# A decoder layer on one core: the second SwiGLU's first two weights split into the places of later sums, the post-norm's load moved behind the weights', two loads moved to the other ring

## The chip, the cores and the metric

The kernel runs on one core of one Trainium2 chip. A core has a matrix engine (PE), three engines for elementwise work (DVE, ACT and POOL), an engine that only issues transfers here (SP) and 16 DMA engines. Each engine works through its own list of instructions in the order of the program and waits where it needs another's result. The metric is the device time of one execution in microseconds, the median of several runs.

## The reference

One decoder layer on x of 512 tokens by 1024, float32: a SwiGLU feed-forward, a mixer of two kinds of recurrent heads, and a second SwiGLU, each between a norm before it and a norm behind it.

```python
x = x + 0.5 * rms_norm(swiglu_ffn(rms_norm(x, norm_pre[l, 0]), ffn1_w_in[l], ffn1_w_out[l]), norm_post[l, 0])
mixed = token_mixer(rms_norm(x, norm_pre[l, 1]), w_mix_in[l], ...)
x = x + rms_norm(mixed, norm_post[l, 1])
x = x + 0.5 * rms_norm(swiglu_ffn(rms_norm(x, norm_pre[l, 2]), ffn2_w_in[l], ffn2_w_out[l]), norm_post[l, 2])

def swiglu_ffn(x, w_in, w_out):
    gate, up = jnp.split(x @ w_in, 2, axis=-1)
    return (jax.nn.silu(gate) * up) @ w_out
```

`w_in` is 1024 by 5632 (gate and up, 2816 columns each), `w_out` 2816 by 1024. The token mixer ends with a product `mix @ w_out` of 1024 by 1024. The result is compared in float32.

## The kernel before

**Precision.** PE multiplies float32 operands in a rounded form (fp32r). Each operand is therefore split into a high part, which is its rounded copy, and a low part, which is the rest. ACT makes the high part (`L273`, 128 x 1024), DVE the low part (`L275`, a subtraction); three matmuls, high by high, high by low and low by high, stand for one. The mixer's output weights are scaled at the same time (`L278` on ACT, `L281` on DVE, two halves of 128 x 512 for each weight).

**Products.** The input product of a SwiGLU is done by a scheme of seven products (p1 to p7) in place of eight for each pair t of column tiles (11 pairs). It works on 2 x 2 blocks: two halves of the tokens, two halves of the contraction, gate and up. A weight has four blocks a, b, c, d of 128 x 1024; some products need sums of blocks, which are made in place in the loaded blocks (`L289`, on POOL for t = 0 of the second SwiGLU, otherwise on DVE). On the other side they need x of the first token half, in two places xq, and sums of x in two more xq and in three places called s. A product is 24 matmuls of 128 x 128 by 128 x 256 on one line, `L602`.

**Weights.** `Layer.weights` takes a list of items, one for each weight that PE will read, in PE's order. An item's blocks are loaded into one of two rings of buffers, `raw` (three places) and `raw2` (five); a load is issued on SP when the place's last reader is done and, unless its group says otherwise, not more than eight items ahead. SP issues loads strictly in order. `split` then makes the item's two parts in one of four places of the tile w; `pull` hands it to a product, and `drop` returns the place. So a weight can be split at most four items ahead. An item may name its own place instead (`dst`); the first SwiGLU does that with three of its first weights, which lie in the s places until the sums come.

**From the mixer to the second SwiGLU.** `mix_out1` is the second half of the mixer's output product: four weights, four token tiles in turn. After each tile come its post-norm, the sum into x and the next pre-norm (square on ACT, `L436`; scale and power on POOL, `L437` and `L441`; the products with the norm's gain on DVE, `L474`, `L484`, `L492`, `L464`). Tiles 0 and 1 are transposed (`L347`) and split into the first token half's x. This much is enough for the first products of the second SwiGLU (`HEADS2`, 14 products p1 and p2 of eight pairs), which PE runs while tiles 2 and 3 are normed, transposed and turned into the sums (`sums`, on `L380` and `L381`). Ten of these 14 products read blocks that are needed again much later; these are loaded once for now (`once`, numbered 0 to 9) and again later. The products are called by p and t: 13 is p1 of pair 3.

`ffn_head` writes the order of this stretch: one split, then two behind the last tile's sum into x, then one behind its norm; then the products, each after the splits that fit. What a p1 product leaves in its bank is copied out (`L629`) before p2 of the same pair adds to the bank; a p5 result is reduced by that copy (`L621`) into the bank that p6 adds to. The context manager `behind` asks the scheduler to issue what it holds after the named instructions. The scheduler sets the final order on each engine; it is fixed when the program is built.

`ffn_out` is the product with `w_out`, in two halves of 512 columns, with the post-norm behind each. It begins with the load of the post-norm's gain (`gpost`, `L152`), whose buffer the mixer's post-norm uses until its last tile.

Of the kernel before, what the change touches and what calls it, by code (L numbers as in the profile page):

```python
# [58 lines left out]
SEQ = (0, 1, 2, 3, 4, 5, 9, 6, 7, 8, 10)  # L59
# [56 lines left out]
class Layer:  # L116
# [108 lines left out]
    def start_loads(self):  # L225

        lds = self.due[-1]
        self.due[-1] = []
        load, self.load = self.load, lambda ld: None
        self.due[-1] = lds  # L230
        self.load_due(-1)
        self.load = load
        return deque(sorted(lds, key=lambda ld: self.first[ld.key]))

    def load(self, ld):
        self.nc.sync.dma_start(self.raw[ld.key], ld.src)

    def lie(self, kind):

# [87 lines left out]
        return w  # L327

    def drop(self, w):
        self.alive -= 1  # L330
        self.free.append(self.slot.pop(id(w))[0])

    def rpow(self, ss, a, b):

# [342 lines left out]
    def ffn_head(self, trans):  # L677


        norm, seen = self.normed, self.col()  # L680
        norm.append(self.nc.gpsimd.tensor_copy(seen, self.hf[:, 17, T - 1 :]))
        self.hold = norm[2:]
        self.full_split()
        with self.behind(*self.added):
            for _ in range(2):
                self.full_split()
        with self.behind(*norm):
            for g in self.copies:
                next(g)
            self.full_split()  # L690
        for n, (p, t) in enumerate(HEADS2):
            if n:
                with self.behind(*([self.lowed] if n > 3 else norm), *([self.copied] if n in (1, 5, 7) else [])):
                    self.feed()
            self.lag()
            self.prod(p, t, False)
            self.after(p, t)
            if n == 0:
                with self.behind(*norm):
                    trans(2)  # L700
            elif n == 2:
                trans(3)
            elif n in (5, 6, 8, 9):
                for g in self.gs:
                    next(g)
        self.hold = ()
        self.holes()
# [149 lines left out]
    def ffn_out(self, gpost_row, scale, after, trans, head):  # L857
# [6 lines left out]
        made = deque((h, None) for h in self.hs)  # L864
# [71 lines left out]
            c = slice(QUARTER * (i // 2), QUARTER * (i // 2 + 1))  # L936
            return [(C[i % 2][v][:, c], slice(QUARTER * v, QUARTER * (v + 1))) for v in range(2)]

        g = self.gain("gpost", gpost_row)
        n = 0  # L940
        for half in range(2):
            C = [[self.ps() for _ in range(2)] for _ in range(2)]
            M, T, left = None, None, len(QUARTERED[half])
            for m, k2 in enumerate(OUT[half][: PAIRS - LAST * half]):
# [10 lines left out]
                else:  # L955
                    w = self.pull()
# [115 lines left out]
    def ffn_items(self, name, w_in, w_out):  # L1072

        made = []
        place = {"p1": "a", "p2": "c", "p3": "d", "p4": "a", "p5": "a", "p6": "a", "p7": "b"}
        place.update({"c1": "a", "c2": "c", "c3": "b", "c4": "d"})
        adds = {}
        second = name == "f2"
        for t in range(1 - second, PAIRS):
            if second:  # L1080
                v1, v3 = SUMS[t]
            elif t >= HEAD:
                v1, v3 = ("p1", t), ("p4", t - 1)
            elif t > 1:
                v1, v3 = ("p2", 2), ("p6", 1)
            else:
                v1, v3 = ("p1", 1), ("p1", 2)
            for at, o, i in ((("p5", t), "a", "d"), (("p6", t), "a", "c"), (v1, "a", "b"), (v3, "b", "d")):
                adds.setdefault(at, []).append(((name, t, o), (name, t, i)))

        def load(t, r, group=None, once=None):
            even = (SEQ.index(t) if second else t) % 2 == 0 and r != "c" if once is None else once > 4
            ring = ("raw", 3) if even else ("raw2", 5)
            k, c = int(r in "cd"), int(r in "bd")
            c0 = c * FF + t * 2 * P
            src = w_in[k * 4 * P : (k + 1) * 4 * P, c0 : c0 + 2 * P].rearrange("(k p) f -> p k f", p=P)
            key = (name, t, r) if once is None else (name, t, r, once)
            return Load(key, src, KH, 2 * P, *ring, 8, group)

        if second:  # L1100
            once = [pt for pt in HEADS2 if pt[1] in ONCE]
            own = {pt: [load(pt[1], place[pt[0]], name if n < 8 else None, n)] for n, pt in enumerate(once)}
            for t in SEQ:
                own[SUMS[t][0]] = own.get(SUMS[t][0], []) + [load(t, r) for r in "abdc"]
            for n, (p, t) in enumerate(ORDER2):
                key = (name, t, place[p]) + ((once.index((p, t)),) if (p, t) in once else ())
                made.append(Item(key, own.get((p, t), ()), None, adds.get((p, t), ())))
        else:
            own = {("p1", t): [load(t, r) for r in "abdc"] for t in range(2, PAIRS)}
            own["c1", 0] = [load(t, r, None if (t, r) == (0, "d") else name) for t in range(2) for r in "acbd"]  # L1110

            stay = {"c1": 2, "c3": 0, "c4": 1}
            for p, t in ORDER:
                if p[0] == "e":
                    continue
                dst = (lambda n=stay[p]: self.stay[n]) if p in stay else None
                made.append(Item((name, t, place[p]), own.get((p, t), ()), None, adds.get((p, t), ()), dst))
        for h in range(2):
            for k2 in OUT[h]:
                src = w_out[k2 * 2 * P : (k2 + 1) * 2 * P, h * 512 : (h + 1) * 512].rearrange("(k p) d -> p k d", p=P)  # L1120
                key = (name, "out", h, k2)
                made.append(Item(key, [Load(key, src, 2, 512, "raw2", 5, 8)], sums=k2 in QUARTERED[h]))
                if k2 in QUARTERED[h]:
                    made.append(Item(key, ()))
                if h == k2 == 0:
                    made.append(Item((name, PAIRS - 1, "a"), ()))
        return made
# [679 lines left out]
```

## Time and profile before

| | us |
|---|---|
| median of 3 runs (942.13 to 942.61) | 942.38 |
| profiled execution, its own time | 941.56 |
| its span, first to last instruction | 939.8 |
| PE busy | 930.5 |
| DVE busy | 772.6 |
| ACT busy | 511.7 |
| POOL busy | 109.6 |

The profiled execution is one run; its time is 1.8 us more than its span, which is what lies around the first and last instruction. Busy times are sums over the engine's instructions. A matmul is counted until its end, though the next one begins before that, so PE's busy share says little of its pace; the starts of matmuls tell it better. In the rows of the timeline stand start, length, engine, line, operation, output and inputs, shape, how many were merged, and in brackets the idle time of the engine before the row with the instruction that ended it. The mean granted clock of PE in this execution is 0.999 of full speed.

### The profile page before, as it was taken

What the parts mean: (1) busy time and instruction counts of PE and PEld (TensorE: products, weight loads), DVE (VectorE), ACT (ScalarE), POOL (GpSimd) and SP (SyncE); (2) the same over time, 40 slices, a digit from 0 to 9 for tenths busy, and PEclk for the clock granted to TensorE, in tenths of its full rate; (3) what the DMA queues carried; (4) which work ended last, traced back from release to release, by engine and by line L of the source; (5) the groups of instructions that cost most, each with busy time, mean ns of one, the idle gap of its engine ahead of it and who ended that gap; (6) DMA issues with size and microseconds to landing.
All of it is one profiled execution on the core that took longest, in us unless ns stands there. A gap on an engine that the chain in (4) does not pass through costs nothing.

```text
span 939.8 us, 18064 instructions
## 1 busy us (share of the span) xinstructions
PE 930.5 (99%) x7471; PEld 895.7 (95%) x7471; DVE 772.6 (82%) x1044; ACT 511.7 (54%) x735; POOL 109.6 (12%) x172
## 2 busy tenths in 40 slices
PE   9999999999999999999999999999999999999997
PEld 7999999999999999998887888899999999999997
DVE  6899988889988886698846664799899989998884
ACT  7645455557456457956532444595455545755541
POOL 3530000000001045200011310314000000000101
PEclk9999999999999999999999999999999999999999
DMA  9242443332342034321212124262444435223212
GB/s 315 90 157 91 131 127 104 105 107 80 114 158 90 24 98 126 94 68 52 84 45 68 46 91 147 75 207 67 133 158 135 135 113 157 91 88 123 83 45 90
DMA packets 86956, 101.35 MB, mean 108 GB/s; under 512 B 4277, under 2 KB 66777, under 8 KB 86874
## 3 DMA queue, kind: packets, MB, share of 16 engines
q1 hardware_dynamic: 86586, 99.68, 33.7%
q8 instruction: 58, 0.95, 0.4%
q10 hardware_dynamic: 288, 0.52, 0.2%
q14 instruction: 24, 0.20, 0.1%
HBM read 98.10 MB, written 2.10 MB: 107 GB/s over the span
## 4 chain that ended last, share of the span: by engine, by line
PE 54%; DVE 3%; issue 2%; DMA 1%; POOL 1%; ACT 1%; POOLq 0%; DVEq 0%; ACTq 0%
PE ps L602 14%; PE ps L892 7%; PE ps L532 6%; PE ps L900 5%; PE ps L179 5%; PE ps L181 5%; PE ps L180 4%; PE ps L1297 2%; DVE w L275 1%; DMA raw<-in_ffn_w_in_dram 1%; PE ps L542 1%; POOL raw L289 1%; DVE raw L289 1%; PE ps L1471 0%; ACT w L273 0%
## 5 line engine op out<-in xcount | busy, mean ns | idle before, releaser
L273 ACT CAST w<-raw 128x1024 fp32r<-128x1024 f32 (+1 forms) x240 | 246.6, 1035 | 230.5 <-PE ps L602 87.3
L275 DVE TENSOR_TENSOR w<-raw,w 128x1024 fp32r<-128x1024 f32 (+1 forms) x240 | 293.8, 1231 | 36.9 <-ACT w L273 36.3
L602 PE MATMUL ps<-xq,w 128*128 128x256 f32 x2064 | 243.8, 277 | 0.7 <-DVE w L275 0.5
L602 PEld LDWEIGHTS ps<-xq,w 128*128 128x128 f32 x2064 | 239.1, 188 | 1.3 <-DVE w L275 0.7
L602 PE MATMUL ps<-sq,w 128*128 128x256 f32 x1512 | 178.0, 276 | 0.6 <-DVE ps L621 0.3
L602 PEld LDWEIGHTS ps<-sq,w 128*128 128x128 f32 x1512 | 174.2, 188 | 1.4 <-ACT ps L653 0.9
L892 PE MATMUL ps<-w,hs 128*128 128x256 f32 x960 | 113.0, 276 | 0.0
L892 PEld LDWEIGHTS ps<-w,hs 128*128 128x128 f32 x960 | 110.7, 188 | 0.0
L289 DVE TENSOR_TENSOR raw<-raw,raw 128x1024 f32<-128x1024 f32 x72 | 89.8, 1251 | 6.9 <-DMA raw<-in_ffn_w_in_dram 5.3
L179 PE MATMUL ps<-w,xq 128*128 128x512 f32 x192 | 78.9, 411 | 0.1
L181 PE MATMUL ps<-w,xq 128*128 128x512 f32 x192 | 74.9, 392 | 0.0
L180 PE MATMUL ps<-w,xq 128*128 128x512 f32 x192 | 74.8, 390 | 0.0
L437 POOL TENSOR_SCALAR col<-col 128x1 f32<-128x1 f32 x24 | 8.7, 362 | 512.8 <-ACT junk L436 512.8
L900 PE MATMUL ps<-w,hs 128*128 128x256 f32 x480 | 57.7, 276 | 0.0
L532 PE MATMUL ps<-xq,w 128*128 128x256 f32 x480 | 56.4, 278 | 0.0
L900 PEld LDWEIGHTS ps<-w,hs 128*128 128x128 f32 x480 | 55.9, 188 | 0.0
L532 PEld LDWEIGHTS ps<-xq,w 128*128 128x128 f32 x480 | 55.2, 188 | 0.5 <-issue 0.5
L179 PEld LDWEIGHTS ps<-w,xq 128*128 128x128 f32 x192 | 36.1, 188 | 8.2 <-issue 0.9
L181 PEld LDWEIGHTS ps<-w,xq 128*128 128x128 f32 x192 | 36.0, 188 | 8.2 <-DVE xq L354 0.3
L811 ACT CAST hs<-hf 128x1024 fp32r<-128x1024 f32 x32 | 33.6, 1051 | 17.5 <-PE ps L900 10.8
L180 PEld LDWEIGHTS ps<-w,xq 128*128 128x128 f32 x192 | 36.2, 188 | 6.7 <-issue 0.2
L812 DVE TENSOR_TENSOR hs<-hf,hs 128x1024 fp32r<-128x1024 f32 x32 | 39.0, 1220 | 1.3 <-ACT hs L811 1.2
(258 smaller groups left out, 1133.3 us busy)
## 6 DMA issues: line engine op xcount, KB each, us to landing
raw<-in_ffn_w_in_dram SPq DMA_DIRECT2D x98, 512.0 KB, 3.7
raw<-in_ffn_w_out_dram SPq DMA_DIRECT2D x44, 512.0 KB, 3.8
raw<-in_w_mix_in_dram SPq DMA_DIRECT2D x28, 512.0 KB, 3.5
raw<-in_w_mix_out_dram SPq DMA_DIRECT2D x8, 512.0 KB, 3.9
out_dram<-xs SPq DMA_DIRECT2D x8, 256.0 KB, 2.0
xs<-in_x_dram SPq DMA_DIRECT2D x6, 256.0 KB, 4.8
gpost<-in_norm_post_dram SPq DMA_DIRECT2D x3, 512.0 KB, 4.1
gpre<-in_norm_pre_dram SPq DMA_DIRECT2D x2, 512.0 KB, 4.7
```

The costliest lines, as they stand in the source:

```text
L179: mm(ps, sh, mh, start=start, stop=False, **kw)
L180: mm(ps, sh, ml, start=False, stop=False, **kw)
L181: mm(ps, sl, mh, start=False, stop=stop, **kw)
L273: nc.scalar.copy(hi, raw)
L275: self.low = nc.vector.tensor_tensor(lo, raw, hi.bitcast(F32), op=ALU.subtract)
L289: (nc.vector if late else nc.gpsimd).tensor_tensor(o, o, c, op=ALU.add)
L532: mm(ps[:, u0:u1], w[:, a, k, :], self.xop(k, b, u0, u1), start=k + n + m == 0, stop=k == ND - 1 and n == 2, skip_group_check=True,)
L602: self.nc.tensor.matmul(ps[:, c], wb[b][:, k, v], left[d][:, k, :], start=first and a + n + k == 0, stop=n == 2 and k == KH - 1, skip_grou ...
L811: self.nc.scalar.copy(hi, src)
L812: self.nc.vector.tensor_tensor(lo, src, hi.bitcast(F32), op=ALU.subtract)
L892: mm(out, a[kk][:, i * P : (i + 1) * P], w[:, b, kk, QUARTER * v : QUARTER * (v + 1)], start=begin and c == kk == n == 0, stop=kk == 1 and ...
L900: mm(ps[:, QUARTER * c : QUARTER * (c + 1)], A[a][:, c], B[b], start=begin and c == n == 0, stop=n == 2, skip_group_check=True,)
```

## The change

- `ffn_items`: the first two items of the second SwiGLU (products 13 and 15) get a `dst`, so they are split into the s places 2 and 0 and not into w. The sums of x are written to the same places later.
- `drop`: an item with a place of its own takes nothing back into the ring.
- `ffn_head`: two splits, not one, are written ahead of the `behind` of the last tile's sum into x; one, not two, in it.
- `load` in `ffn_items`: of the loads numbered `once`, 5, 6 and 9 use `raw` and 7 and 8 use `raw2`; before, 5 to 9 used `raw`. The loads that are not in the group of early loads are 7 and 8, before 8 and 9.
- `ffn_out`: in the second SwiGLU the load of `gpost` is put behind the last load issued so far (`self.loaded`, which `load` now keeps).

```diff
     def load(self, ld):
-        self.nc.sync.dma_start(self.raw[ld.key], ld.src)
+        self.loaded = self.nc.sync.dma_start(self.raw[ld.key], ld.src)
...
     def drop(self, w):
-        self.alive -= 1
-        self.free.append(self.slot.pop(id(w))[0])
+        if id(w) in self.slot:
+            self.alive -= 1
+            self.free.append(self.slot.pop(id(w))[0])
...
         self.hold = norm[2:]
-        self.full_split()
+        for _ in range(2):
+            self.full_split()
         with self.behind(*self.added):
-            for _ in range(2):
-                self.full_split()
+            self.full_split()
...
-        g = self.gain("gpost", gpost_row)
+
+        with self.behind(*([self.loaded] if self.second else [])):
+            g = self.gain("gpost", gpost_row)
...
-            even = (SEQ.index(t) if second else t) % 2 == 0 and r != "c" if once is None else once > 4
+            even = (SEQ.index(t) if second else t) % 2 == 0 and r != "c" if once is None else once in (5, 6, 9)
...
-            own = {pt: [load(pt[1], place[pt[0]], name if n < 8 else None, n)] for n, pt in enumerate(once)}
+            own = {pt: [load(pt[1], place[pt[0]], None if n in (7, 8) else name, n)] for n, pt in enumerate(once)}
...
-                made.append(Item(key, own.get((p, t), ()), None, adds.get((p, t), ())))
+
+                dst = (lambda n=2 * (n == 0): self.stay[n]) if n < 2 else None
+                made.append(Item(key, own.get((p, t), ()), None, adds.get((p, t), ()), dst))
```

In the order of instructions that the scheduler makes of it, the counts on every engine stay the same. On ACT and DVE the first of the two splits stands between the splits of the mixer's third and fourth output weights, the second behind the fourth's. On PE one matmul of the second token tile of `mix_out1` moves ahead of five of the first. On SP the load of `gpost` moves from before the second of the weights loaded for pair 1 to behind the seventh load of `w_out`, and the loads of weights 28 and 16 stand ahead of those of pair 1. In w the places of all later items of the second SwiGLU are shifted by two in the round of four.

## The prediction, made before the changed kernel was run

> **What bounds the kernel now.** I read the page's first part, then the matmul engine's timeline over the stretch that the change touches (end of the mixer's output product, head of the second SwiGLU), then ACT, DVE, POOL and the DMA queue over the same stretch.
>
> ```profile
> span 939.8 us, 18064 instructions
> PE 930.5 (99%) x7471; PEld 895.7 (95%) x7471; DVE 772.6 (82%) x1044; ACT 511.7 (54%) x735; POOL 109.6 (12%) x172
> ...
> L602 PE MATMUL ps<-xq,w 128*128 128x256 f32 x2064 | 243.8, 277 | 0.7 <-DVE w L275 0.5
> ```
>
> PE is busy for 930.5 of 939.8 us, so only 9.3 us of shown idle can be won in the whole program, most of it elsewhere. A change that moves no matmul can gain only what PE loses near it.
>
> ```profile
> 605.54 2.05 PE L602 MATMUL ps<-xq,w 128*128 128x256 f32 x16
> 608.08 1.21 PE L602 MATMUL ps<-xq,w 128*128 128x256 f32 x8 [0.49 <-DVE w L275]
> 609.13 1.03 PE L347 MATMUL ps<-ident,xn 128*128 128x128 f32 x8
> ...
> 616.36 11.46 PE L602 MATMUL ps<-xq,w 128*128 128x256 f32 x96
> 628.07 24.95 PE L602 MATMUL ps<-xq,w 128*128 128x256 f32 x216 [0.26 <-ACT hf L629]
> 652.86 11.04 PE L602 MATMUL ps<-sq,w 128*128 128x256 f32 x96
> 663.74 2.88 PE L602 MATMUL ps<-xq,w 128*128 128x256 f32 x24
> ...
> 683.35 2.99 PE L602 MATMUL ps<-sq,w 128*128 128x256 f32 x24 [0.35 <-DVE ps L621]
> ```
>
> These are PE's merged timeline rows: start, length, line, output and inputs, count, and in brackets the idle time before them with its releaser. The undisturbed pace comes from 652.86 to 663.74: 10.88 us for 96 matmuls, 0.113 us each; a whole product (24 matmuls) is 2.72 us. A row's length contains the 0.277 us of its last matmul (page, L602), though the next could have followed 0.113 us after that one's start, so a wait costs about 0.16 us more than the bracket shows. Restarting costs some more: from 608.08 to 609.13 eight matmuls take 1.05 us for 0.91, and I take 0.11 for each restart. So the three waits cost:
> - at 608.08, the low part of the first product's weight (L275): 0.49 + 0.16 + 0.11 = 0.76 us;
> - at 628.07, the copy L629 of a p1 bank: 0.26 + 0.16 + 0.11 = 0.53 us;
> - at 683.35, DVE's L621: 0.35 + 0.16 + 0.11 = 0.62 us.
>
> Together 1.91 us. The rest of 605 to 690 runs within a few ns per matmul of full pace. These three are the stake.
>
> **The change, part by part.**
>
> *The first two weights are split early, into the s places.* Today their splits (L273 on ACT, L275 on DVE) stand behind the norms of the mixer's last token tiles, because they need slots of the w ring. In the changed order of instructions they stand earlier: the first between the splits of the mixer's third and fourth output weights (L278 and L281, two each), the second right behind the fourth's.
>
> ```profile
> 581.46 2.11 ACT L278 ACTIVATE w<-raw,prm 128x512 fp32r<-128x512 f32 x3 [1.51 <-PE ps L181]
> 583.58 0.60 ACT L436 ACTIVATE junk<-ps 128x512 f32<-128x512 f32 x1
> ...
> 603.09 1.03 ACT L273 CAST w<-raw 128x1024 fp32r<-128x1024 f32 x1
> ...
> 622.81 0.58 ACT L381 CAST sq<-ps 128x512 fp32r<-128x512 f32 x1
> 624.57 1.05 ACT L273 CAST w<-raw 128x1024 fp32r<-128x1024 f32 x1 [1.17 <-DMA raw<-in_ffn_w_in_dram]
> ...
> 627.42 0.60 ACT L629 COPY hf<-ps 128x512 f32<-128x512 f32 x1
> ```
> ```profile
> 582.22 2.13 DVE L281 SCALAR_TENSOR_TENSOR w<-raw,prm,w 128x512 fp32r<-128x512 f32 x3 [1.43 <-ACT w L278]
> 584.30 0.69 DVE L474 TENSOR_TENSOR y<-ps,gpost 128x512 f32<-128x512 f32 x1
> 584.91 0.75 DVE L281 SCALAR_TENSOR_TENSOR w<-raw,prm,w 128x512 fp32r<-128x512 f32 x1
> ...
> 606.82 1.21 DVE L275 TENSOR_TENSOR w<-raw,w 128x1024 fp32r<-128x1024 f32 x1
> ...
> 625.65 1.23 DVE L275 TENSOR_TENSOR w<-raw,w 128x1024 fp32r<-128x1024 f32 x1 [0.93 <-ACT w L273]
> ```
> ```profile
> 579.19 0.37 SPq L236 DMA_DIRECT2D raw<-in_ffn_w_in_dram  x1
> raw<-in_ffn_w_in_dram SPq DMA_DIRECT2D x1, 512.0 KB, 3.7
> 608.10 0.37 SPq L236 DMA_DIRECT2D raw<-in_ffn_w_in_dram  x1
> 608.67 0.35 SPq L152 DMA_DIRECT2D gpost<-in_norm_post_dram  x1
> ...
> 619.47 0.37 SPq L236 DMA_DIRECT2D raw<-in_ffn_w_in_dram  x1
> ```
>
> The last fence holds DMA issues, and for the load issued at 579.19 its 3.7 us to landing: the first product's weight is there at 582.9. Before, it waits till 603.09 to be split; after, it is ready by 586 and PE's 0.76 us at 608 goes. Nothing new gates that product: DVE is done with its x when it turns to the L275 at 606.82.
>
> The price is paid in the mixer's output product. Split into steps on ACT: the two L278 of the third weight end at 582.9 (581.46 plus two at 0.71); the new L273 runs 583.0 to 584.0; the square L436, now at 583.58, follows to 584.6; the fourth weight's two L278 end at 585.4 and 586.1. On DVE: two L281 end at 583.6; the new L275 waits for ACT and runs 584.1 to 585.3; L474 takes it to 585.9 (0.61, from 584.30 to 584.91); the fourth weight's two L281 end at 586.6 and 587.3, where now they end near 584.35 and 585.66. PE wants them here:
>
> ```profile
> 586.04 0.39 PE L179 MATMUL ps<-w,xq 128*128 128x512 f32 x1
> 586.27 0.39 PE L180 MATMUL ps<-w,xq 128*128 128x512 f32 x1
> ...
> 586.95 0.39 PE L180 MATMUL ps<-w,xq 128*128 128x512 f32 x1
> ```
>
> L179 at 586.04 needs the first high half (ready 585.4), L180 at 586.27 the first low half, L180 at 586.95 the second low half. In the changed order one matmul of the next token tile (0.23 us) stands ahead of the first L180, which moves these to 586.50 and 587.18. So PE waits about 0.15 us at the first, restarts (0.1), and the second is then in time: 0.25 us lost. From below this could be nothing, if those reads are a little faster; from above it is the load's landing that decides (rivals). The norms behind shift by 0.2 to 0.4 us. PE now takes their transposes without a wait (no bracket at 609.13), so I cost that at nothing; with no cover it would be those 0.2 to 0.4.
>
> The later sums of x overwrite the two places. Their first write is the L381 at 622.81, 13 us after the first product has been read; the second place's comes later still. No wait is added.
>
> *Two more weights ahead, and the two loads in the other ring.* With two weights outside the four-slot ring, each later split may be made two products sooner. Today ACT waits 1.17 us at 624.57 for a load issued at 619.47, because that load (product 16's weight) waits for a place of the three-deep ring; this delays L629 to 627.42, which is the 0.53 us at 628.07. After, weights 28 and 16 take the places in the five-deep ring that the first two splits free at 585 and 588, and are there some 20 us sooner. Following ACT's rows in the changed order, without that wait, L629 comes at about 625.5. PE, 0.76 - 0.25 us ahead by then, wants it at 627.1 (628.07 less the 0.42 of the wait and these 0.51). The 0.53 goes.
>
> *The post-norm's load moves.* It stands at 608.67 between two weight loads, 512 KB like each of them; after, it follows the seventh load of w_out.
>
> ```profile
> 817.88 0.37 SPq L236 DMA_DIRECT2D raw<-in_ffn_w_out_dram  x1
> 876.00 0.42 DVE L474 TENSOR_TENSOR y<-ps,gpost 128x256 f32<-128x256 f32 x1
> ```
>
> That load is issued at 817.88 and its first reader is at 876.00, 58 us later. Cost nothing; if that cover were gone it would be one landing, 3.7 us. At 608 it frees one load's transfer for weights that PE does not wait for: nothing by itself.
>
> *The third stall.* DVE hardly pauses from 625.65 until it stands still 2.87 us before 665.92, and is late for PE at 683.
>
> ```profile
> 644.96 3.30 DVE L289 TENSOR_TENSOR raw<-raw,raw 128x1024 f32<-128x1024 f32 x1
> 649.73 3.37 DVE L275 TENSOR_TENSOR w<-raw,w 128x1024 fp32r<-128x1024 f32 x1 [0.20 <-ACT w L273]
> ...
> 665.92 1.23 DVE L289 TENSOR_TENSOR raw<-raw,raw 128x1024 f32<-128x1024 f32 x1 [2.87 <-DMA raw<-in_ffn_w_in_dram]
> ...
> 682.60 0.69 DVE L621 TENSOR_TENSOR ps<-ps,hf 128x512 f32<-128x512 f32 x1
> ```
> ```profile
> 600.22 0.55 POOL L441 TENSOR_TENSOR col<-col,nhalf 128x1 f32<-128x1 f32 x1
> ...
> 606.96 1.47 POOL L441 TENSOR_TENSOR col<-col,nhalf 128x1 f32<-128x1 f32 x1
> ...
> 649.61 2.41 POOL L289 TENSOR_TENSOR raw<-raw,raw 128x1024 f32<-128x1024 f32 x1 [2.43 <-DVE w L275]
> ```
> ```profile
> 661.32 0.37 SPq L236 DMA_DIRECT2D raw<-in_ffn_w_in_dram  x1
> ```
>
> The 2.87 us at 665.92 is a load issued at 661.32, when a DVE split freed its place, and used 4.6 us later. All of this is DVE's chain, so it moves with DVE. Two L275 (1.13 us pace each) leave 606 to 612, and the 0.93 us at 625.65 goes: 3.2 us at most. The tile-3 norm and PE's release of slots hold some back; I follow it to 2.0 us. From below it is PE's own shift, 0.76 + 0.53 - 0.25 = 1.04, since the slots come free that much sooner. The wait at 683 vanishes once DVE is 1.04 + 0.51 = 1.6 us earlier. At 2.0 it does, so 0.62 more.
>
> Sum: -0.76 - 0.53 - 0.62 + 0.25 = -1.66 us. The profiled execution took 941.56 us (span 939.8); it becomes 939.9. It stood 0.82 under the median of the three runs, so the median goes from 942.38 to 940.7.
>
> [...]
>
> **Rivals.**
> 1. *The load is late and the mixer stalls.* For: ACT's new L273 sits 0.1 us behind a landing at 582.9, with nothing between. Every microsecond later goes to PE in full, beyond 0.25. Against: the queue is empty when that load is issued. The slowest landing in these rows is 5.1 us (issued 619.47, read at 624.57): +1.4 us, which leaves a gain of 0.3 (942.1). It decides for slower by 0.2% only if the load is 3.5 us late (1.66 + 1.88).
> 2. *DVE gains only PE's shift.* Then 0.5 us of wait stays at 683: gain 1.1, 941.3.
> 3. *Slower: POOL's additions collide with DVE's splits.* POOL's L441 takes 0.55 us alone (600.22) and 1.47 beside a DVE L275 (606.96); the DVE rows at 644.96 and 649.73 take 3.3 us for 1.2, the second beside the POOL addition of 649.61. [...] So two of POOL's four additions are fully hit today. If the new phase let the other two hit as well, DVE would lose 2 x 2.1 = 4.2 us, its lead of 2.0 would become a lag of 2.2, and PE would end 2.2 us later: 944.6. It decides when more than one further addition is hit. Against: the order on DVE between the first addition and the last is the same in both.
> 4. *More than the sum.* The 96 matmuls from 616.36 to 628.07 take 11.71 us, 0.83 over pace, and the wait is 0.53 of that; the other 0.3 falls where loads follow each other on the queue (608.10 to 619.47). If fewer loads there cure it and the mixer's 0.25 is nothing: 2.2 us gained, 940.2.
> 5. *It does nothing,* because the waits only move to another line. 942.4. Against: three waits have three causes, and two are removed outright.
>
> **How the numbers follow.** The forecast 0.45, its own range 940.3 to 941.0; rival 2 0.17, 4 0.15, 1 0.09, 3 0.07, 5 0.07. What a measurement can tell from no change is 0.2%, 1.88 us: faster means below 940.50, slower above 944.26. The forecast lies 0.2 us from that bound, so a third of it (0.15) and all of rival 4 count as faster, with a little of rival 2: 0.31. Rival 3 and a very late load make slower 0.08; 0.61 is the same. The range runs from rival 4 with a run's spread, 939.8, to beyond rivals 1 and 5, 942.8.
>
> **What will show it.** Right: two splits into s places near 583 and 586; at most 0.3 us of PE's wait there; no wait of PE near 608 and 628; no DMA wait of ACT near 624; the addition chain on POOL 1 to 2 us earlier; no wait on L621 near 683. Wrong: PE waiting on L281 near 586 for over 0.5 us; more DVE rows of 3.3 us; a new wait of PE in 690 to 818, where DVE is nearly full; or a slower pace of the two products that read their weights from the s places.

## The result, and the profile after

The changed kernel takes 940.17 us (median of 13 runs, 939.2 to 941.33), the kernel before 942.46 (13 runs, 941.37 to 943.83): a ratio of 0.9976, 95% interval 0.9967 to 0.9985. That is 2.3 us faster, between 1.4 and 3.1. The forecast was 940.7, a gain of 1.66, which lies inside the interval; the measured median lies 0.5 us below it. It also lies below 940.50, where the prediction let "faster" begin; to that it had given 0.31, and 0.61 to the same. The interval reaches to both sides of that bound of 1.88 us, so the times alone do not settle which of the two it is. The profiled execution took 940.18 us.

The first part of the page of the changed kernel:

```profile
span 938.5 us, 18056 instructions
PE 930.2 (99%) x7471; PEld 895.9 (95%) x7471; DVE 772.4 (82%) x1044; ACT 511.9 (55%) x735; POOL 107.4 (11%) x172
```

PE's timeline of the changed kernel over the stretch of the three stalls (start, length, line, count; these lines of the code are one higher than before, so `L603` answers to `L602`, `L622` to `L621`, `L630` to `L629`; in dve_extra and load_late they are shifted by one and two more):

```profile
606.29 2.98 PE L603 MATMUL ps<-xq,sq 128*128 128x256 f32 x24
...
609.90 3.08 PE L603 MATMUL ps<-xq,sq 128*128 128x256 f32 x24
...
616.39 35.84 PE L603 MATMUL ps<-xq,w 128*128 128x256 f32 x312
...
682.03 2.88 PE L603 MATMUL ps<-sq,w 128*128 128x256 f32 x24
```

No row has a bracket any more: the waits that stood at 608.08, 628.07 and 683.35 are gone, and what was two rows from 616.36 to 652.86 (96 and 216 matmuls) is one of 312. The first two products read `sq`, the s places. On ACT and DVE the two early splits stand where the order put them:

```profile
582.12 1.41 ACT L278 ACTIVATE w<-raw,prm 128x512 fp32r<-128x512 f32 x2 [1.54 <-PE ps L181]
583.50 1.05 ACT L273 CAST sq<-raw 128x1024 fp32r<-128x1024 f32 x1
...
585.04 1.32 ACT L278 ACTIVATE w<-raw,prm 128x512 fp32r<-128x512 f32 x2
586.26 1.04 ACT L273 CAST sq<-raw 128x1024 fp32r<-128x1024 f32 x1
...
625.74 0.61 ACT L630 COPY hf<-ps 128x512 f32<-128x512 f32 x1
```
```profile
584.59 1.23 DVE L275 TENSOR_TENSOR sq<-raw,sq 128x1024 fp32r<-128x1024 f32 x1 [0.27 <-ACT sq L273]
...
586.33 1.40 DVE L281 SCALAR_TENSOR_TENSOR w<-raw,prm,w 128x512 fp32r<-128x512 f32 x2
...
664.36 1.23 DVE L289 TENSOR_TENSOR raw<-raw,raw 128x1024 f32<-128x1024 f32 x1 [2.12 <-DMA raw<-in_ffn_w_in_dram]
...
681.04 0.69 DVE L622 TENSOR_TENSOR ps<-ps,hf 128x512 f32<-128x512 f32 x1
```

The copy at 625.74 is no longer behind a wait for a load, and the L622 that PE waited for at 683 comes at 681.04, not 682.60 (2.19 us sooner when both are counted from the row at 570 below).

**The yardstick.** Times of whole executions scatter by 2 us, more than the terms in question. Two rows of PE's timeline lie ahead of the change and behind its effects. Of the kernel before and of the changed one:

```profile
570.08 0.50 PE L179 MATMUL ps<-w,xq 128*128 128x512 f32 x1
...
766.36 3.91 PE L602 MATMUL ps<-sq,w 128*128 128x256 f32 x32
```
```profile
570.71 0.50 PE L179 MATMUL ps<-w,xq 128*128 128x512 f32 x1
...
764.95 5.28 PE L603 MATMUL ps<-sq,w 128*128 128x256 f32 x44
```

From the first start to the second it is 196.28 us before and 194.24 after: 2.04 us gained in this stretch. (The two spans differ by only 1.3, since this execution of the changed kernel was already 0.63 us later at 570, ahead of everything that was changed. From the second row to the end both take 173.5 us.) The expectations below measure from 8.8 us later to 0.4 us earlier; their 187.12 and 185.07 are the same two lengths less 9.17.

### The profile page after: what moved, and what is told of

It reads as the page before. It is cut to its first block, busy times and chain, and to the rows that moved or that the text cites. A ratio compares the mean times of both kernels' runs of the same rounds, so it can differ in the third digit from the quotient of the medians.

```text
span 938.5 us, 18056 instructions
## 1 busy us (share of the span) xinstructions
PE 930.2 (99%) x7471; PEld 895.9 (95%) x7471; DVE 772.4 (82%) x1044; ACT 511.9 (55%) x735; POOL 107.4 (11%) x172
## 4 chain that ended last, share of the span: by engine, by line
PE 63%; ACT 1%; issue 0%; DVE 0%; DVEq 0%; POOLq 0%; POOL 0%; ACTq 0%
PE ps L603 22%; PE ps L893 7%; PE ps L533 6%; PE ps L901 5%; PE ps L179 5%; PE ps L181 5%; PE ps L180 5%; PE ps L1302 2%; PE ps L543 1%; PE ps L348 1%; PE ps L1476 0%; PE ps L1387 0%; PE ps L1583 0%; PE ps L1556 0%; PE ps L1342 0%; PE ps L1580 0%
## 5 line engine op out<-in xcount | busy, mean ns | idle before, releaser
L603 PE MATMUL ps<-xq,w 128*128 128x256 f32 x2016 | 237.1, 277 | 0.0
L603 PEld LDWEIGHTS ps<-xq,w 128*128 128x128 f32 x2016 | 232.9, 188 | 0.0
L603 PE MATMUL ps<-sq,w 128*128 128x256 f32 x1512 | 177.9, 276 | 0.3
L603 PEld LDWEIGHTS ps<-sq,w 128*128 128x128 f32 x1512 | 174.3, 188 | 0.9 <-ACT ps L654 0.9
L533 PE MATMUL ps<-xq,w 128*128 128x256 f32 x480 | 56.4, 278 | 0.0
L533 PEld LDWEIGHTS ps<-xq,w 128*128 128x128 f32 x480 | 55.2, 188 | 0.5 <-issue 0.5
```

What stands on the lines that cost most here:

```text
L533: mm(ps[:, u0:u1], w[:, a, k, :], self.xop(k, b, u0, u1), start=k + n + m == 0, stop=k == ND - 1 and n == 2, skip_group_check=True,)
L603: self.nc.tensor.matmul(ps[:, c], wb[b][:, k, v], left[d][:, k, :], start=first and a + n + k == 0, stop=n == 2 and k == KH - 1, skip_grou ...
```

## The experiments

All are told by one table. Each run's profile gives the stretch, and PE's losses in it, from the starts of single matmuls: the distance between two starts less the regular one (0.113 us for 256 columns, 0.227 for 512), taken over the wait and the matmul behind it. "Wide" is a series of matmuls at a spacing of 117 to 118 ns in place of 113 (last section). "Lead" is how much earlier than in the kernel before DVE begins the L621 of the stall at 683, counted from the row at 570. All in us.

| run | stretch | mixer, 587 | 608 | wide, 616 on | 628 | 683 | wide, other | sum of losses | lead |
|---|---|---|---|---|---|---|---|---|---|
| before | 196.28 | 0 | 0.76 | 0.25 | 0.53 | 0.62 | 0 | 2.16 | 0 |
| before_again | 196.10 | 0 | 0.79 | 0.24 | 0.13 | 0.65 | 0.14 | 1.95 | 0.19 |
| gpost_only | 196.43 | 0 | 0.79 | 0 | 0.68 | 0.79 | 0 | 2.26 | -0.14 |
| rings_only | 195.98 | 0 | 0.79 | 0 | 0 | 0.47 | 0.55 | 1.81 | 0.96 |
| places_only | 195.15 | 0.25 | 0 | 0 | 0 | 0.79 | 0 | 1.04 | 1.15 |
| places_and_gpost | 195.52 | 0.19 | 0 | 0 | 0 | 0.64 | 0.55 | 1.38 | 1.34 |
| places_and_rings | 194.53 | 0.39 | 0 | 0 | 0 | 0 | 0 | 0.39 | 2.00 |
| after (all three) | 194.24 | 0.10 | 0 | 0 | 0 | 0 | 0 | 0.10 | 2.19 |
| after_again | 194.30 | 0.16 | 0 | 0 | 0 | 0 | 0 | 0.16 | 2.22 |
| dve_extra | 195.63 | 0.17 | 0 | 0 | 0 | 1.33 | 0 | 1.50 | 0.67 |
| split_late | 194.12 | 0 | 0 | 0 | 0 | 0 | 0 | 0 | 2.18 |
| load_late | 195.04 | 0 | 0.98 | 0 | 0 | 0 | 0 | 0.98 | 1.35 |
| third_place | 194.40 | 0 | 0 | 0 | 0 | 0.27 | 0 | 0.27 | 1.89 |

Stretch less losses is 194.06 to 194.17 in all thirteen, so nothing else in the stretch moved by more than 0.11 us.

### One part at a time

places_only has the `dst`, the guard in `drop` and the order of splits; rings_only the ring and group of the numbered loads; gpost_only the move of the post-norm's load; places_and_gpost and places_and_rings leave one part out. In the changed kernel's terms:

```diff
# places_and_gpost: the rings as before
-            even = (SEQ.index(t) if second else t) % 2 == 0 and r != "c" if once is None else once in (5, 6, 9)
+            even = (SEQ.index(t) if second else t) % 2 == 0 and r != "c" if once is None else once > 4
...
-            own = {pt: [load(pt[1], place[pt[0]], None if n in (7, 8) else name, n)] for n, pt in enumerate(once)}
+            own = {pt: [load(pt[1], place[pt[0]], name if n < 8 else None, n)] for n, pt in enumerate(once)}
# places_and_rings: the load as before
-        with self.behind(*([self.loaded] if self.second else [])):
-            g = self.gain("gpost", gpost_row)
+        g = self.gain("gpost", gpost_row)
```

> The kernel before, with the first two weights split into the s places and the order of splits that goes with it; rings and the post-norm's load as before. Theory 1 (each part removes its own stall): the 0.76 us at 608 goes and the mixer loses 0.1, while weight 16 still waits for a place of the three-deep ring, so that ACT waits for its load near 624 and PE for the copy near 628 (0.5 to 1.1 us, PE being earlier): a gain of 0 to 0.7 us, ratio 0.9993 to 1.000. Theory 2 (the two weights outside the ring of four bring every later split and so every later load forward, and the rings add nothing): no stall at 608, 628 and 683, a gain of 1.9 to 2.3 us, ratio 0.9976 to 0.998.

> The kernel before, with only the two loads in the other ring. Theory 1: ACT no longer waits for the load near 624, PE's 0.53 us at 628 goes, the 0.76 at 608 stays, and DVE gains the 0.93 us that it waited at 625.65, which PE's shift and the wait at 683 (1.04 together) just use up: a gain of 0.5 to 1.1 us, ratio 0.9988 to 0.9995. Theory 2: the place in the ring of five comes free only when the first two weights are split, near 603 to 606, so the load is hardly earlier and the stall at 628 stays: a gain of 0 to 0.2 us, ratio 0.9998 to 1.000.

> The kernel before, with only the post-norm's load behind the last weight load. Theory 1 (it is worth nothing): all three stalls stay, a gain within 0.1 us, and the matmuls from 616 to 623 keep their slow spacing of 117 to 118 ns. Rival (fewer transfers at that time let PE run at full pace, or bring weight 16's load forward): the spacing from 616 to 623 falls to 113 ns or the wait of ACT near 624 falls from 1.17 us to below 0.3: a gain of 0.25 to 0.8 us, ratio 0.9992 to 0.9997.

> The changed kernel with the two loads back in their old ring. Theory 1: the stall at 628 comes back (0.5 to 1.1 us) with ACT's wait for the load near 624, and DVE loses about 1 us of its lead, so that the wait at 683 comes back in part (0.2 to 0.6): 0.7 to 1.7 us slower than the changed kernel, ratio 0.9983 to 0.9995. Theory 2: as fast as the changed kernel, ratio 0.9976 to 0.998. If the post-norm's load matters for weight 16's, it is faster than the places alone by up to 0.5 us.

> The changed kernel with the post-norm's load back in its old place among the weights' loads. Theory 1 (the move is worth nothing): the stretch from the mixer's second tile to the last stall before 766 is as long as in the changed kernel (185.1 us, less than 0.1 us apart if the matmuls' spacing is the same), no stall at 608, 628 and 683, and the time is the changed kernel's within 0.5 us. Rival (the load delays weights by one transfer, 1.7 us, and DVE, whose lead at 683 is only some 0.25 us more than PE needs, falls behind): a stall near 683 of 0.3 to 0.8 us.

Measured, with the ratio to the kernel before (the recorded ratios differ by up to 0.0008 from the quotients of the medians): places_only 942.17 us, 0.9985 (0.9976 to 0.9995); rings_only 941.01, 0.9988 (0.9977 to 1.0); gpost_only 942.59, 0.9997 (0.9988 to 1.0006); places_and_gpost 941.7, 0.9981 (0.9973 to 0.999), all four beside 942.9 us for the kernel before; places_and_rings 940.17 beside 942.15, 0.9982 (0.9973 to 0.999). The intervals overlap too much to rank the parts; the stretches do it.

Both theories were partly wrong. The stall at 608 goes with the places. The stall at 628 goes with the places alone and with the rings alone; the places do not take away ACT's wait, they only put the copy far enough ahead of PE (56.00 us behind the row at 570, where it was 57.34 in the kernel before). The stall at 683 goes only with both. Of places_only, PE's rows at 616 and 683 and ACT's wait near 624:

```profile
617.83 35.84 PE L603 MATMUL ps<-xq,w 128*128 128x256 f32 x312
...
684.16 3.00 PE L603 MATMUL ps<-sq,w 128*128 128x256 f32 x24 [0.52 <-DVE ps L622]
```
```profile
625.18 1.05 ACT L273 CAST w<-raw 128x1024 fp32r<-128x1024 f32 x1 [0.77 <-DMA raw<-in_ffn_w_in_dram]
...
628.03 0.60 ACT L630 COPY hf<-ps 128x512 f32<-128x512 f32 x1
```

Of rings_only, PE's rows at the same two places:

```profile
618.69 35.84 PE L602 MATMUL ps<-xq,w 128*128 128x256 f32 x312
...
684.70 3.10 PE L602 MATMUL ps<-sq,w 128*128 128x256 f32 x24 [0.20 <-DVE ps L621]
```

Here lies the rings' share: ACT's 0.77 us hold its splits up and DVE's behind them. With the places but without the rings DVE leads by 1.15 and 1.34 us, with both by 2.00 to 2.22; that is worth the 0.64 to 0.79 of PE's time at 683. The post-norm's load is worth nothing: gpost_only loses 0.10 more than before, and places_and_rings differs from the changed kernel by the 0.29 us in the mixer alone. One sign that the expectation gave to its rival did come, the spacing of 113 ns from 616 to 623 in gpost_only. The move of the load is not its reason: the spacing is the same in rings_only, places_only and places_and_rings, where that load stays, and gpost_only gained no time by it, since its stalls at 628 and 683 were larger.

The columns 683 and lead belong together. Up to 683 the kernel before loses 1.54 us; a run that loses x there has PE 1.54 - x ahead, and then 0.62 + (1.54 - x) - lead should remain of the stall. It gives 0.41 for rings_only (0.47 measured), 0.76 for places_only (0.79), 0.63 for places_and_gpost (0.64), 0.83 for gpost_only (0.79), 0.67 for before_again (0.65), and -0.13 and -0.22 for the two executions of the changed kernel, which have no stall. So the third stall is a race between PE and DVE. That the sizes fit is bookkeeping, as soon as PE waits there for this instruction alone; the test is that the stall is there in the eight executions whose remainder is positive and gone in the five where it is not. The 0.62 contains the 0.11 of a restart, which goes too when no wait is left, so the race is won once the remainder is below 0.11. The margin is read from the rows: where there is a stall, PE's matmul follows the end of DVE's L621 by 0.05 us, and in the changed kernel by 0.30 and in after_again by 0.40. The changed kernel wins the race by 0.25 and 0.34 us.

### The margin at 683

```diff
             elif n in (5, 6, 8, 9):
                 for g in self.gs:
                     next(g)
+            elif n == 10:
+                with self.behind(self.low):
+                    for _ in range(6):
+                        self.nc.vector.tensor_tensor(self.extra, self.ident[:, :64], self.ident[:, 64:], op=ALU.add)
```

> The changed kernel with six additions of 128 x 64 on DVE between 630 and 645, which nobody reads: at most 0.8 us of DVE time. Theory A (PE waits at 683 as soon as DVE's lead over its place in the kernel before is less than PE's lead plus 0.51; the traces put the lead at 2.20 and the need at 1.95): a stall at 683 of about 0.55 us, no other. Theory B (the 0.89 us that DVE itself waits for PE before 660.42 take the extra work up): no stall at 683, and the time is the changed kernel's.

`extra` is a tile of 128 x 64 that nothing reads. 941.38 us, ratio 0.9993 (0.9984 to 1.0002). PE's row, then DVE's and POOL's, of dve_extra:

```profile
683.05 3.00 PE L604 MATMUL ps<-sq,w 128*128 128x256 f32 x24 [1.06 <-DVE ps L623]
```
```profile
639.46 0.21 DVE L711 TENSOR_TENSOR extra<-ident 128x64 f32<-128x64 f32 x1
...
642.00 3.15 DVE L711 TENSOR_TENSOR extra<-ident 128x64 f32<-128x64 f32 x4
...
665.62 1.23 DVE L290 TENSOR_TENSOR raw<-raw,raw 128x1024 f32<-128x1024 f32 x1 [3.59 <-DMA raw<-in_ffn_w_in_dram]
```
```profile
642.16 2.39 POOL L290 TENSOR_TENSOR raw<-raw,raw 128x1024 f32<-128x1024 f32 x1 [3.70 <-DVE w L276]
```

Theory A holds: the stall is back, and Theory B's cover is not there. But the stall is 1.33 us (the formula gives 1.32) and not 0.55, since the 0.8 us for the added work were an estimate that no run had shown: the six additions took 3.5. Four additions take 3.15 us where one takes 0.21: one of them ran into POOL's addition of 642.16 and took some 2.4 (the six have a mean of 0.578, the five others 0.21 each), as long as that. Delayed splits then issued the load before 665.62 later, by 1.0 us when counted from the row at 570, and its reader began 0.55 us longer after the issue (5.34 us for 4.80). DVE's wait for it grew from 2.12 to 3.59, and the lead fell by 1.5 us. An addition of 1024 columns fared alike in this execution: the L290 at 650.01 took 3.31 us beside POOL's of 648.76 (3.47), and the one at 646.32, beside none, 1.23.

In third_place, which is split_late with the third product's weight in the last s place, the same margin was lost:

```diff
-                dst = (lambda n=2 * (n == 0): self.stay[n]) if n < 2 else None
+                dst = (lambda n=(2, 0, 1)[min(n, 2)]: self.stay[n]) if n < 3 else None
```

> The kernel with the first early split behind half of the mixer's fourth weight, and the third product's weight in the last free s place too. Theory (PE now loses nothing that DVE's lead could give back): PE as in that kernel, stretch 184.95 to 185.05 us, DVE's lead at 683 larger by 0 to 0.6 us; against the kernel before a ratio of 0.997 to 0.9985. Rival (the sums of x now wait for the third product, or the new place shifts the splits against POOL's additions): a stall of PE between 612 and 690 of 0.3 us or more.

940.75 us, ratio 0.9982 (0.9973 to 0.9991). The stretch is 194.40, and 0.27 us of the stall are back. Neither reason of the rival shows: the sums wait for nothing new and POOL's additions lie as before. Nor does the theory hold, since the lead shrank. Of third_place, DVE and the issue of the load that it waits for, and that issue in the changed kernel:

```profile
666.15 1.23 DVE L289 TENSOR_TENSOR raw<-raw,raw 128x1024 f32<-128x1024 f32 x1 [2.52 <-DMA raw<-in_ffn_w_in_dram]
```
```profile
661.00 0.37 SPq L236 DMA_DIRECT2D raw<-in_ffn_w_in_dram  x1
```
```profile
659.56 0.37 SPq L236 DMA_DIRECT2D raw<-in_ffn_w_in_dram  x1
```

DVE waited 2.52 us for the load, 0.4 longer than in the changed kernel; the lead is 1.89, and the formula gives 0.27. The third place did not delay the issue: counted from the row at 570 it came 0.05 us sooner than in the changed kernel. The load itself was slower: its reader begins 5.15 us after the issue, for 4.80 there. In the thirteen executions this time is 4.60 to 5.34 us, so it may well be scatter, but one execution of third_place does not show whether it would come again.

### The price in the mixer

```diff
-        for _ in range(2):
-            self.full_split()
+        with self.behind(self.last_high, self.last_low):
+            for _ in range(2):
+                self.full_split()
```

`last_high` and `last_low` are the last `L278` and `L281` written so far; the scheduler then puts the first early split behind the first half of the mixer's fourth weight.

> The changed kernel with the first early split behind half of the mixer's fourth weight, on ACT and on DVE, and no longer in front of all of it. Theory (the 0.10 us that PE loses at 587 is that weight's low half waiting for the split): the 0.10 us is gone, the first product at 606 still has its weight in time (it is split by 589), and the stretch to 766 is 184.95 us for 185.07. Rival (the second half now waits longer): PE loses 0.2 to 0.5 us near 588. By the times alone neither can be told from the changed kernel.

> The changed kernel, unchanged, for one more execution with a profile. No stall at 608, 628 and 683 as before; PE's loss in the mixer between 0.0 and 0.4 us and equal, within 0.05, to DVE's wait for the first early split less some 0.16 (the profiles so far have 0.27 and 0.10, 0.33 and 0.11, 0.39 and 0.19, 0.42 and 0.25, 0.56 and 0.39), since the landing of that weight varies. Stretch 184.95 to 185.4 us, or up to 0.55 more if a restart leaves the matmuls at 117 to 118 ns.

split_late: 940.25 us, ratio 0.9981 (0.9972 to 0.9989); no loss near 587, stretch 194.12, the shortest of all (184.95 as the expectation measures it). By its time it cannot be told from the changed kernel. So the 0.10 us is the fourth weight standing behind the early split. What PE gains there it takes from the margin at 683: the end of DVE's instruction and PE's matmul are only 0.16 us apart, which leaves 0.11. after_again: 940.21 us, DVE's wait 0.34 and PE's loss 0.16, where the expectation's rule gives 0.18. The expectation's pair 0.33 and 0.11, which is dve_extra, is 0.33 and 0.17 by the starts of the matmuls, so all six pairs follow the rule within 0.04. How much PE loses depends on when the load lands. In places_and_rings ACT had to wait for it, and PE lost 0.39:

```profile
583.75 1.05 ACT L273 CAST sq<-raw 128x1024 fp32r<-128x1024 f32 x1 [0.26 <-DMA raw<-in_ffn_w_in_dram]
```
```profile
raw<-in_ffn_w_in_dram SPq DMA_DIRECT2D x1, 512.0 KB, 3.9
```

The second fence is the first of the loads that begin near 579.8, issued at 579.81 there: 3.9 us to its landing at 583.7, and the split begins right behind.

To make the load late, I issued it as the fourth of its group. A load of the group is issued at 571.1 already, so by the trace this is the third of those that begin at 579.9, where the changed kernel has it first:

```diff
-        for ld in sorted(lds, key=lambda ld: self.first[ld.key]):
-            self.load(ld)
+        late = ("f2", 3, "a", 0)
+        for ld in sorted(lds, key=lambda ld: self.first[ld.key] + 2.5 * (ld.key == late)):
+            with self.behind(*([self.loaded] if ld.key == late else [])):
+                self.load(ld)
```

> The changed kernel with the first product's weight as the fourth and not the second of the loads that begin at 579.8, which delays its landing by two transfers, some 3 us; the scheduler puts its split behind half of the mixer's fourth weight. Theory (the first rival of the prediction: ACT and DVE take their instructions in order, so the mixer's weight waits for the load and PE for it, nearly microsecond for microsecond): PE waits 2 to 3.5 us near 588, the time is 2 to 3.5 us over the changed kernel's, which is slower than the kernel before by 0 to 1.2. Rival (the wait is covered, or something lets the mixer's weight pass): less than 0.3 us of wait there.

940.7 us, ratio 0.9984 (0.9975 to 0.9993). There is no wait near 588, which is the rival's sign, but neither theory was put to the test. Of load_late, ACT and PE:

```profile
584.87 0.71 ACT L280 ACTIVATE w<-raw,prm 128x512 fp32r<-128x512 f32 x1
587.41 2.00 ACT L275 CAST sq<-raw 128x1024 fp32r<-128x1024 f32 x2 [1.83 <-DMA raw<-in_ffn_w_in_dram]
```
```profile
608.03 2.15 PE L605 MATMUL ps<-xq,sq 128*128 128x256 f32 x16 [0.70 <-DVE xq L372]
```

The scheduler put the split behind the whole of the fourth weight, and not behind half of it as expected, so the mixer lost nothing. What waited behind the 1.83 us on ACT, and 2.13 on DVE, was the norm of the next token tiles, and PE paid for that 21 us later: 0.98 us at 608, where x of the second tile was late. The first rival's price of a microsecond for a microsecond in the mixer was therefore not tried beyond 0.4 us. Up to there it holds: from the changed kernel to places_and_rings DVE's wait for the split grew by 0.29 us, and PE's loss by 0.29.

### The kernel before once more

> The kernel before, unchanged, for one more execution with a profile. Theory C (the slow spacing of 117 to 118 ns after a wait of PE is chance, settled anew at each restart): the three stalls stay within 0.2 us of 0.76, 0.53 and 0.62, while the matmuls from 616 to 623, slow in one of the ten profiles so far, run at 113 ns here, or others at another restart run slow; the stretch from the mixer's second tile to the stall near 766 is 0.2 to 0.3 us shorter than 187.12 if none is slow. Theory D (it belongs to the program): the same 55 matmuls are slow again.

941.81 us. The three stalls are there, but the one at 628 is 0.13 and not 0.53, outside the 0.2 of theory C: ACT's split waits for PE at that point, and no longer for the load.

```profile
624.60 1.05 ACT L273 CAST w<-raw 128x1024 fp32r<-128x1024 f32 x1 [0.78 <-PE ps L602]
```

The load was there at least 0.39 us sooner than in the execution shown first (1.17 less 0.78), so this stall is worth 0.13 to 0.68 from one execution to the next (0.68 is gpost_only). The 55 matmuls at 117 to 118 ns after 616 came again, as theory D had it. Some 31 others ran slow as well, near 636, where PE had not waited, so not at a restart as theory C has it.

## Why the prediction was right, and where it was wrong

- **What bounds the kernel, and the stall at 608.** Right. It was worth 0.76 to 0.79 in the executions without the places, and it is gone with them.
- **The stall at 628.** Gone, as forecast, with the copy at 625.74 (forecast 625.5; counted from the row at 570 it came 0.4 us sooner than that). Its cause was put too narrowly: it did not need the other ring and the earlier load, since the places alone remove it, as the rings alone do. Its size of 0.53 was one draw between 0.13 and 0.68.
- **The stall at 683.** Gone. The lead was taken as 2.0 and measured 2.19; the need was taken as 1.6 and was 1.95 (1.44 + 0.51), because PE was further ahead than the sum had it (1.44, not 1.04). Right with 0.25 us to spare, not 0.4; a load that took 0.35 us longer, as in third_place, lost it again.
- **The price in the mixer, 0.25.** The mechanism was right, the size too high for the changed kernel: 0.10 and 0.16. In the first of these PE's matmul starts on time and only the step behind it is 0.10 longer, which is the sum's restart without its wait of 0.15. The forecast's 0.25 lies within the 0.10 to 0.39 of the executions with this order of splits, so the size is set by when the load lands. The working had the right load, the first of the row at 579.19, and the right landing: issue to landing is 3.6 us in the changed kernel (forecast 3.7).
- **The post-norm's load: nothing.** Right.
- **The sum.** It missed the term that rival 4 had, 0.25 us of wide spacing between 616 and 623, and the mixer's price was 0.15 less: -1.66 - 0.25 - 0.15 = -2.06, and the stretch shows -2.04. This comes near rival 4's case, a gain of 2.2; that its 940.2 us was met to 0.1 is partly luck, as the interval of the measured gain is 1.4 to 3.1. Its reason was wrong: fewer loads cured nothing. What set the spacing is open (last section), so these 0.25 us of the gain cannot be put down to a part of the change. Stretches behind 616 in the kernel before, in gpost_only and in the changed kernel (length; busy time of PE, PEld, DVE, ACT, POOL; granted clock; DMA share; GB/s):

```profile
616.40:619.20 2.80, 2.80 (x26) 2.80 (x25) 2.71 (x3) 2.80 (x6) 0.00 (x0) 1.00 0.67 205
```
```profile
618.70:621.50 2.80, 2.80 (x27) 2.80 (x26) 2.70 (x4) 2.80 (x6) 0.00 (x0) 1.00 0.69 205
```
```profile
624.70:627.40 2.70, 2.70 (x26) 2.70 (x25) 2.70 (x5) 2.50 (x5) 0.00 (x0) 1.00 1.01 332
```

  Matmuls are some 118 ns apart at a DMA share of 0.67 before, and 113.3 at 0.69 and the same 205 GB/s in gpost_only and at 1.01 after. So in these rows the spacing does not follow the load on the DMA engines.
- **Rivals 1, 2, 3 and 5.** A late load did not stall the mixer by more than 0.4 us in any run. DVE gained 2.19, more than PE's shift of 1.44. POOL's additions hit the same two DVE instructions, 1.7 us earlier (at 643.21 and 647.99, 3.30 and 3.36 us for 1.2). The waits did not move elsewhere: the table has no other loss, and behind 766 both kernels take 173.5 us.

## What to carry to other kernels

A stall that is a race between two engines goes only when the second engine gains more than the first, so before several stalls are added up, ask how much earlier each repair makes the engine that waits at the next one: here the third was won by a quarter of a microsecond. A small change is better read from two fixed rows of the trace than from the time, and its parts from the same rows with one part taken away. Work put ahead of something that PE needs soon makes that thing wait for the work's own load: here 0.10 to 0.39 us, by the landing, and nothing where half of what PE needed stood first.

## What was not expected of the hardware

In the thirteen executions PE's matmuls of 256 columns ran at one of two spacings, at a granted clock of 0.998 to 1.00: 113.3 ns, or 117.7. Once it was there, the wider one held for tens or hundreds of matmuls (31 near 636 in before_again, 375 in the mixer). Most of these series began right behind a wait of PE or behind a change of shape without one, such as the transposes ahead of 616 in the kernel before; the one near 636 in before_again began behind neither. Rows of the same 48 and 43 matmuls behind the stall at 683, of rings_only and of gpost_only:

```profile
688.45 5.92 PE L602 MATMUL ps<-sq,w 128*128 128x256 f32 x48
694.21 5.23 PE L602 MATMUL ps<-xq,w 128*128 128x256 f32 x43
```
```profile
689.44 5.72 PE L602 MATMUL ps<-sq,w 128*128 128x256 f32 x48
695.00 5.04 PE L602 MATMUL ps<-xq,w 128*128 128x256 f32 x43
```

The 0.20 us for 48 are 4.2 ns each; all the matmuls at the wider spacing there cost 0.55 us, as much as a stall. In this stretch every series of over 50 matmuls at the wider spacing ended in a p1 product, in which some ten of the 24 matmuls are 116 to 122 ns apart in any case. The largest case lies in the mixer, which the change does not touch. Of third_place and of split_late:

```profile
355.75 16.42 PE L533 MATMUL ps<-xq,w 128*128 128x256 f32 x138
```
```profile
355.92 16.26 PE L533 MATMUL ps<-xq,w 128*128 128x256 f32 x142
```

That is 117.8 ns against 113.3 (the last matmul's 0.28 us taken off). In four of the thirteen profiled executions (places_only, rings_only, gpost_only, third_place) 375 matmuls between 355 and 405 had the wider spacing, some 1.6 us, and their spans are the longest four, 940.7 to 942.3. In these four the row at 570 comes at 572.0 to 572.4, in the others at 570.1 to 570.9; so for these thirteen it is a large part of why the spans scatter. The 55 after 616 came in both executions of the kernel before and in none of the eleven others; whether that belongs to its order of instructions or is chance is open, and so is the cause of the two spacings.
